# Differential attention: logits as float32 products over 64 rows instead of split products over 128

## The chip, the cores and the metric

The kernel runs on one core of a Trainium2 chip. The metric is the device time of one execution in microseconds (us); smaller is better. TensorE (PE) multiplies, VectorE (DVE) and ScalarE (ACT) work on tiles and empty PSUM, GpSimd (POOL) copies, and the queue of SyncE (SP) issues DMAs.

## The reference, cut to what matters

Two blocks run one after the other on x of 512 tokens by 1024 features, all in float32. The second block has two layers; its second layer is a differential attention with 8 heads of two sides each, a side having 64 features:

```python
q = q.reshape(B, S, B_HEADS, 2, HEAD_DIM_2) * (HEAD_DIM_2 ** -0.5)   # 8 heads, 2 sides, 64 features
k = k.reshape(B, S, B_HEADS, 2, HEAD_DIM_2)
v = v.reshape(B, S, B_HEADS, 2 * HEAD_DIM_2)
...
logits = jnp.einsum('bqhjd,bkhjd->bhjqk', q_blk, k).astype(jnp.float32) + bias[None]
p = jax.nn.softmax(logits, axis=-1)
a = p[:, :, 0] - lam_full * p[:, :, 1]
return jnp.einsum('bhqk,bkhe->bqhe', a.astype(v.dtype), v)
...
o = rms_norm(o, subln_g) * (1.0 - lambda_init)
```

For each head, side and tile of 128 queries the logits are a product of 128 by 512 over only 64 features.

## The kernel before

The stages follow one another: `mix`, `mlp1`, `A`, `mlpA`, `B`, `mlpB`. The change is in `B`, the function `layer_b`. Activations lie feature-major (128 features by 512 tokens in a tile). The precise products are made of fp32r pieces: `split` writes a value's fp32r copy (hi) and the rest (lo), and `mm3` adds hi*hi, hi*lo and lo*hi. The weights come as blocks in a fixed order (`_plan`, a class `Stream` with `take`); a block of 256 columns is loaded by the SP queue into `raw` (two buffers) and split by ACT (`hi`, L251) and DVE (`lo`, L252) into two pieces of 128 columns. `project` makes one tile of 128 columns by 512 tokens with 24 such products (`ps_pj`, three PSUM banks).

Everything else that PE writes in the layer (logits, transposes, attention output) takes its bank from one pool of five (`pwt`, tag `w`). Per head `hh` the steps are:

- `proj` (q, k, v; one block is two heads). DVE empties the bank with the norm's scale. A q tile is split (ACT L1338, DVE L1339) so that one half of the 128 rows holds a side's hi and the other half its lo. A k tile is split and copied so that both halves hold the side's hi (`KH`, ACT L1351 and POOL L1352) or its lo (`KL`, DVE L1353 and POOL L1354). v is turned token-major by PE (`ps_tm`).
- `soft`: for each of four query tiles and two sides, two products of 128 rows into one bank (`ps_lgb`: KH, then KL added). DVE adds the bias and takes the row's minimum while it empties the bank (L1378; q carries a minus sign), ACT takes the exponent with row sums (L1380), then reciprocal and scales (L1382, L1383), ACT scales side 1 (L1384) and DVE adds both sides (L1385). The bias tiles `bt` (448 KB each, three buffers) come by the SP queue (L1364).
- `pvb`: 16 transposes of the weights (`ps_aT`), copies by DVE and ACT, 16 products with v (`ps_ob`), squares on ACT (L1413), a reciprocal root of a dozen small DVE operations (L400 to L410) and a scaling by DVE (`ob`, L1417).
- `turn_out`: 4 transposes of `ob` (`ps_obT`), then a split by ACT (L279, `mh`) and DVE (L280, `ml`).

`B_STEPS` lists the steps in program order (q, k, v with the block number, s, p, t with the head). A scheduler turns it into one order per engine, fixed at build time: the earlier step goes first among those that it believes ready, so that projection products also stand between the pieces of other steps. On the chip each engine follows its order and waits on semaphores.

In layer `A` (`softmax_pair`, L1053) the logits are already float32 products over 64 rows, two heads in turn: per query tile 192, 256, 256 and 192 columns in the first three pairs of heads and 128 columns in the other five.

Of the kernel before, what the change touches and what calls it, by code (L numbers as in the profile page):

```python
# [16 lines left out]
P = 128  # L17
T = 512
# [9 lines left out]
A_STEPS = "q0 k0 s0 v0 t0 q1 p0 k1 s1 v1 t1 q2 p1 k2 s2 q3 t2 k3 s3 v2 t3 a0 p2 v3 p3".split()  # L28
B_STEPS = ("q0 k0 s0 v0 s1 p0 q1 t0 p1 k1 t1 s2 v1 s3 p2 q2 t2 p3 k2 t3 s4 v2 s5 p4 q3"
           " t4 p5 k3 t5 s6 s7 v3 p6 p7 t6 t7").split()  # L30
OH_B, OH_1, OH_2, OH_3 = 0, 1024, 1408, 1664
# [26 lines left out]
def _plan():  # L58
# [14 lines left out]
    for l, nm, steps in ((0, "a", A_STEPS), (1, "b", B_STEPS)):  # L73
        for t in steps:
            if t[0] in "qkv":
                out.append(_w_cols(nm + "_w_qkv_2", 0, {"q": 0, "k": 1024, "v": 2048}[t[0]] + int(t[1]) * 256))
        out += _w_out(nm + "_w_o_2", 0, 0, D)
        for half in range(2):
            out += [_w_cols("mlp_w_in_2", l, c) for c in range(half * 2048, (half + 1) * 2048, 256)]
            out += _w_out("mlp_w_out_2", l, half * 2048, (half + 1) * 2048)  # L80
# [89 lines left out]
def build(nc, tc, a, out, phases=("mix", "mlp1", "A", "mlpA", "B", "mlpB")):  # L170
# [814 lines left out]
    def rev(ap):  # L985

        return bass.AP(ap.tensor, ap.offset + P - 1, [list(ap.ap[0]), [P, 4], [-1, P]])
# [306 lines left out]
    def layer_b(st, biasd):  # L1294
# [24 lines left out]
        M_["evac"] = None  # L1319
        qs, ks, vs, at, ob = {}, {}, {}, {}, {}  # L1320

        def proj(i2, nm):
            wb = ws.take()
            for i in range(2):
                hh = 2 * i2 + i
                ps = project(wb[i:i + 1], x)  # L1330
                t = sp.tile([P, T], F32, tag="sq", name=nm)
                if nm == "q":
                    V.scalar_tensor_tensor(out=rev(t), in0=v4(ps), scalar=-0.125, in1=v4(st.rs), op0=ALU.mult,
                                           op1=ALU.mult)
                    qs[hh] = [gp.tile([P, T], F32R, tag="Q", name="Q", bufs=5) for _ in range(2)]
                    for j in range(2):
                        n, o = half[j], half[1 - j]
                        act(out=qs[hh][j][n, :], in_=t[n, :], func=AF.Copy)  # L1338
                        V.tensor_tensor(out=qs[hh][j][o, :], in0=t[n, :], in1=qs[hh][j][n, :].bitcast(F32),  # L1339
                                        op=ALU.subtract)  # L1340
                    continue
                V.tensor_tensor(out=t, in0=ps, in1=st.rs, op=ALU.mult)
                if nm == "v":
                    vs[hh] = gp.tile([P, T], F32, tag="vt", name="vt", bufs=4)
                    token_major(vs[hh], t)
                    continue
                kh = [gp.tile([P, T], F32R, tag=f"KH{j}", name="KH", bufs=2) for j in range(2)]
                kl = [(gp, sp)[j].tile([P, T], F32R, tag=("KL", "hold")[j], name="KL", bufs=2) for j in range(2)]
                for j in range(2):
                    n, o = half[j], half[1 - j]  # L1350
                    act(out=kh[j][n, :], in_=t[n, :], func=AF.Copy)  # L1351
                    G.tensor_copy(kh[j][o, :], t[n, :])  # L1352
                    V.tensor_tensor(out=kl[j][n, :], in0=t[n, :], in1=kh[j][n, :].bitcast(F32), op=ALU.subtract)  # L1353
                    G.tensor_copy(kl[j][o, :], kl[j][n, :].bitcast(F32))  # L1354
                ks[hh] = (kh, kl)

        half = (slice(0, 64), slice(64, P))

        def soft(hh):
            kh, kl = ks[hh]  # L1360
            bt = []
            for j in range(2):
                b = gp.tile([P, 896], F32, tag="bt", name="bt", bufs=3)
                nc.sync.dma_start(b, bass.AP(bv.tensor, bv.offset + (2 * hh + j) * OH_N + OH_B, [[1, P], [1, 896]]))  # L1364
                bt.append(b)
            mn = sp.tile([P, 2, 4], F32, tag="bmn", name="bmn")
            ss = sp.tile([P, 2, 4], F32, tag="bss", name="bss")
            rc = sp.tile([P, 2, 4], F32, tag="brc", name="brc")
            A = []
            for t in range(4):  # L1370
                Lt = []
                ts = slice(t * P, (t + 1) * P)
                for j in range(2):
                    ps = pwt("ps_lgb")
                    mm(ps, qs[hh][j][:, ts], kh[j], True, False)
                    mm(ps, qs[hh][j][:, ts], kl[j], False, True)
                    L = gp.tile([P, T], F32, tag=f"L{j}", name="Lb", bufs=8 if j == 0 else 2)
# [9 lines left out]
                A.append(Lt[0])  # L1387
            at[hh] = A

# [40 lines left out]

        for step in B_STEPS:
            nm, n = step[0], int(step[1])
            if nm in "qkv":
                proj(n, nm)
            elif nm == "s":
                soft(n)
            elif nm == "p":
                pvb(n)
            else:
                turn_out(n)  # L1440
# [177 lines left out]
```

## Time and profile before

| | us |
|---|---|
| time, median of 3 runs | 1919.89 |
| the runs | 1911.01 to 1925.99 |
| the profiled execution's own time | 1911.74 |
| its span, first to last instruction | 1910.0 |

The profile is of one execution. Busy times are sums over instructions; a PE record's end is modelled and reaches into the next one, so that the pace of PE is read from one start to the next. A float32 product shows as two records (two passes), an fp32r product and a transpose as one. The idle time of an engine stands in brackets with what ended it.

### The profile page before, as it was taken

To read this page: it belongs to the slowest core of one execution; us is meant where nothing else is said; L and a number is where in the kernel's file an instruction comes from. 1 tells how busy PE (TensorE), PEld (TensorE's weight loads), DVE (VectorE), ACT (ScalarE), POOL (GpSimd) and SP (SyncE) were. 2 spreads that over 40 slices of the span, in tenths; PEclk is the share of its full clock that TensorE was granted. 3 is DMA by queue.
4 is the path that set the end of the run, shared out by engine and by line. 5 is a ranking of instruction groups with operands and counts; after the bars stand their busy time and mean duration, and the time that the engine had idled before them with its cause. 6 is when DMAs were issued, how large, how long until landed. Compare 5 with 4: busy or idle time off the path is not lost.

```text
span 1910.0 us, 23525 instructions
## 1 busy us (share of the span) xinstructions
PE 1875.1 (98%) x9219; PEld 1541.2 (81%) x9219; DVE 1110.6 (58%) x2109; ACT 765.3 (40%) x1350; POOL 143.1 (7%) x136
## 2 busy tenths in 40 slices
PE   7999999999999999999999999999999999999997
PEld 5887878788888887787888888888888888888886
DVE  6795756666356666568543344457877754334433
ACT  5533334344234444354332134336656543213322
POOL 1232210011001103000000000001111000000000
PEclk9999999999999999999999999999999999999999
DMA  5231213222332234222332222343222222322221
GB/s 192 79 116 56 71 48 121 90 94 73 104 110 100 71 116 145 79 80 83 107 108 89 101 98 89 133 138 109 102 82 86 94 100 89 108 91 91 108 89 44
DMA packets 39646, 185.53 MB, mean 97 GB/s; under 512 B 9055, under 2 KB 10847, under 8 KB 22000
## 3 DMA queue, kind: packets, MB, share of 16 engines
q1 hardware_dynamic: 37552, 177.45, 26.6%
q0 software_dynamic: 1984, 6.59, 1.0%
q8 instruction: 72, 1.18, 0.2%
q14 instruction: 38, 0.31, 0.0%
HBM read 176.31 MB, written 7.71 MB: 96 GB/s over the span
## 4 chain that ended last, share of the span: by engine, by line
PE 55%; DVE 3%; ACT 1%; issue 1%; DVEq 0%; ACTq 0%
PE ps_pj L188 49%; PE ps_ob L188 1%; PE ps_lgb L188 1%; PE ps_po L188 1%; PE ps_aT L1396 1%; ACT junk L1413 0%; PE ps_lg L188 0%; DVE lo L252 0%; PE ps_bc L188 0%; DVE KL L1353 0%; DVE nb L408 0%; DVE nb L409 0%; PE ps_obT L1425 0%; PE ps_pT L1149 0%; PE ps_mean L188 0%
## 5 line engine op out<-in xcount | busy, mean ns | idle before, releaser
L188 PE MATMUL ps_pj<-xh,hi 128*128 128x512 f32 x1504 | 592.2, 394 | 11.9 <-ACT hi L251 11.0
L188 PE MATMUL ps_pj<-xl,hi 128*128 128x512 f32 x1504 | 590.9, 393 | 0.0
L188 PE MATMUL ps_pj<-xh,lo 128*128 128x512 f32 x1504 | 590.5, 393 | 0.0
L251 ACT ACTIVATE hi<-raw 128x1024 fp32r<-128x1024 f32 (+2 forms) x308 | 317.2, 1031 | 635.0 <-PE ps_pj L188 595.8
L252 DVE TENSOR_TENSOR lo<-raw,hi 128x1024 fp32r<-128x1024 f32 (+2 forms) x308 | 370.4, 1204 | 301.8 <-ACT hi L251 300.7
L188 PEld LDWEIGHTS ps_pj<-xh,hi 128*128 128x128 f32 x1504 | 283.1, 188 | 70.7 <-ACT hi L251 11.2
L188 PEld LDWEIGHTS ps_pj<-xh,lo 128*128 128x128 f32 x1504 | 283.1, 188 | 58.2 <-DVE lo L252 1.1
L188 PEld LDWEIGHTS ps_pj<-xl,hi 128*128 128x128 f32 x1504 | 283.2, 188 | 56.8 <-DVE xl L280 0.6
L188 PE MATMUL ps_pj<-ah,lo 128*128 128x512 f32 (+1 forms) x704 | 271.0, 385 | 0.0
L188 PE MATMUL ps_pj<-al,hi 128*128 128x512 f32 (+1 forms) x704 | 270.7, 385 | 0.2 <-DVE al L277 0.2
L188 PE MATMUL ps_pj<-ah,hi 128*128 128x512 f32 (+1 forms) x704 | 270.9, 385 | 0.0
L188 PEld LDWEIGHTS ps_pj<-al,hi 128*128 128x128 f32 x704 | 132.3, 188 | 26.8 <-DVE al L277 0.5
L188 PEld LDWEIGHTS ps_pj<-ah,hi 128*128 128x128 f32 x704 | 132.3, 188 | 26.5 <-ACT ah L276 0.4
L188 PEld LDWEIGHTS ps_pj<-ah,lo 128*128 128x128 f32 x704 | 132.3, 188 | 26.0
L469 DVE TENSOR_TENSOR ot<-ps_pj,r 128x512 f32<-128x512 f32 x31 | 21.5, 692 | 108.1 <-PE ps_pj L188 108.1
L188 PE MATMUL ps_pj<-mh,hi 128*128 128x512 f32 x192 | 74.8, 394 | 1.0 <-ACT mh L276 0.9
L276 ACT ACTIVATE ah<-ms 128x512 fp32r<-128x512 f32 x64 | 40.4, 632 | 87.4 <-DVE ms L974 86.0
L188 PE MATMUL ps_pj<-ml,hi 128*128 128x512 f32 x192 | 74.4, 392 | 0.6 <-DVE ml L277 0.6
L188 PE MATMUL ps_pj<-mh,lo 128*128 128x512 f32 x192 | 74.0, 390 | 0.0
L277 DVE TENSOR_TENSOR al<-ms,ah 128x512 fp32r<-128x512 f32 x64 | 44.3, 692 | 45.0 <-ACT ah L276 45.0
L947 DVE SCALAR_TENSOR_TENSOR my<-ms,cols,my 128x511 f32<-128x511 f32 (+1 forms) x88 | 65.6, 748 | 2.8 <-ACT my L945 1.3
L1380 ACT ACTIVATE Lb<-Lb,bmn 128x512 f32<-128x512 f32 x64 | 45.6, 713 | 13.9 <-DVE bmn L1378 11.6
(341 smaller groups left out, 1880.8 us busy)
## 6 DMA issues: line engine op xcount, KB each, us to landing
raw<-w_all SPq DMA_DIRECT2D x137, 1024.0 KB
bt<-biasd SPq DMA_DIRECT2D x16, 448.0 KB
raw<-w_all SPq DMA_DIRECT2D x8, 768.0 KB
raw<-w_all SPq DMA_DIRECT2D x8, 640.0 KB
hscr<-h POOLq DMA_DIRECT2D x16, 256.0 KB, 2.4
hold<-hscr SPq DMA_DIRECT2D x16, 256.0 KB
hs<-x_t SPq DMA_DIRECT2D x8, 256.0 KB
hold<-x_t SPq DMA_DIRECT2D x8, 256.0 KB
```

What stands on the lines that cost most here:

```text
L188: return nc.tensor.matmul(o, lhsT=l, rhs=r, start=start, stop=stop)
L251: act(out=hv, in_=iv, func=AF.Copy)
L252: i_lo = V.tensor_tensor(out=lv, in0=iv, in1=hv.bitcast(F32), op=ALU.subtract)
L276: act(out=dst_hi, in_=src, func=AF.Copy)
L277: V.tensor_tensor(out=dst_lo, in0=src, in1=dst_hi.bitcast(F32), op=ALU.subtract)
L469: V.tensor_tensor(out=t, in0=ps, in1=scale_row, op=ALU.mult)
L947: V.scalar_tensor_tensor(out=y[:, jj:], in0=s[:, :T - jj], scalar=col(base + m), in1=y[:, jj:], op0=ALU.mult, op1=ALU.add)
L1380: act(out=L, in_=L, func=AF.Exp, scale=-1.0, bias=mn[:, j, t:t + 1], accum_out=ss[:, j, t:t + 1])
L1396: nc.tensor.transpose(ps[:, t * P:(t + 1) * P], A[t][:, kt * P:(kt + 1) * P], ident)
```

## The change

`q` and `k` are no longer split. DVE writes them from PSUM straight into float32 tiles (`Q`, `K`, four buffers each), and each logit tile is one float32 product over the 64 rows of its side: side 0 lies on rows 0 to 63, side 1 on rows 64 to 127. The products of two query tiles form a group of four, the sides in turn, in a written order (`chain`), which stands behind the projection product issued last before it in program order (`in_order`; orders on PE, no semaphores). `soft` is cut in two (`s`: query tiles 0 and 1, `u`: 2 and 3), `proj` into its two tiles (`a`, `b`), and `B_STEPS` puts groups between them. The order of the weight blocks stays. ACT's and DVE's work on the logits is the same.

```diff
-B_STEPS = ("q0 k0 s0 v0 s1 p0 q1 t0 p1 k1 t1 s2 v1 s3 p2 q2 t2 p3 k2 t3 s4 v2 s5 p4 q3"
-           " t4 p5 k3 t5 s6 s7 v3 p6 p7 t6 t7").split()
+B_STEPS = ("q0a q0b k0a k0b s0 v0a u0 v0b s1 p0 q1a u1 q1b t0 p1 k1a k1b t1 s2 v1a u2 v1b s3 p2 q2a u3 q2b t2 p3"
+           " k2a k2b t3 s4 v2a u4 v2b s5 p4 q3a u5 q3b t4 p5 k3a s6 k3b t5 u6 v3a s7 v3b u7 p6 p7 t6 t7").split()
...
-        def proj(i2, nm):
-            wb = ws.take()
-            for i in range(2):
+        def proj(i2, nm, tile_):
+            if tile_ == "a":
+                wts[nm] = ws.take()
+            for i in ("ab".index(tile_),):
                 hh = 2 * i2 + i
-                ps = project(wb[i:i + 1], x)
-                t = sp.tile([P, T], F32, tag="sq", name=nm)
+                ps = project(wts[nm][i:i + 1], x)
                 if nm == "q":
-                    V.scalar_tensor_tensor(out=rev(t), in0=v4(ps), scalar=-0.125, in1=v4(st.rs), op0=ALU.mult,
+                    qs[hh] = gp.tile([P, T], F32, tag="Q", name="Q", bufs=4)
+                    V.scalar_tensor_tensor(out=rev(qs[hh]), in0=v4(ps), scalar=-0.125, in1=v4(st.rs), op0=ALU.mult,
                                            op1=ALU.mult)
-                    qs[hh] = [gp.tile([P, T], F32R, tag="Q", name="Q", bufs=5) for _ in range(2)]
-                    for j in range(2):
-                        n, o = half[j], half[1 - j]
-                        act(out=qs[hh][j][n, :], in_=t[n, :], func=AF.Copy)
-                        V.tensor_tensor(out=qs[hh][j][o, :], in0=t[n, :], in1=qs[hh][j][n, :].bitcast(F32),
-                                        op=ALU.subtract)
...
+                elif nm == "k":
+                    ks[hh] = gp.tile([P, T], F32, tag="K", name="K", bufs=4)
+                    V.tensor_tensor(out=ks[hh], in0=ps, in1=st.rs, op=ALU.mult)
...
-                    act(out=kh[j][n, :], in_=t[n, :], func=AF.Copy)
-                    G.tensor_copy(kh[j][o, :], t[n, :])
-                    V.tensor_tensor(out=kl[j][n, :], in0=t[n, :], in1=kh[j][n, :].bitcast(F32), op=ALU.subtract)
-                    G.tensor_copy(kl[j][o, :], kl[j][n, :].bitcast(F32))
...
+            for t in (2 * part, 2 * part + 1):
                 Lt = []
-                ts = slice(t * P, (t + 1) * P)
+                if t % 2 == 0:
+                    lg, seq = [], []
+                    for u in (t, t + 1):
+                        for j in range(2):
+                            lg.append(pwt("ps_lgb"))
+                            seq.append(mm(lg[-1], q[half[j], u * P:(u + 1) * P], k[half[j], :]))
+                    chain(seq)
+                    in_order(before, seq[0])
                 for j in range(2):
-                    ps = pwt("ps_lgb")
-                    mm(ps, qs[hh][j][:, ts], kh[j], True, False)
-                    mm(ps, qs[hh][j][:, ts], kl[j], False, True)
+                    ps = lg.pop(0)
```

`before` is PE's last projection product when `soft` is called. The two `bt` tiles of a head are requested in part 0 and used until the end of part 1.

## Rows read from the trace of the kernel before

**Rows 1.** The page, its part on busy time (us, share of the span, instructions) and the head of the chain that ended last.

```profile
PE 1875.1 (98%) x9219; PEld 1541.2 (81%) x9219; DVE 1110.6 (58%) x2109; ACT 765.3 (40%) x1350; POOL 143.1 (7%) x136
...
PE 55%; DVE 3%; ACT 1%; issue 1%; DVEq 0%; ACTq 0%
```

**Rows 2.** Stretches of layer B, each two heads long: length, then busy time of PE, its weight loads, DVE, ACT and POOL (instructions in brackets), granted clock, DMA share and GB/s.

```profile
1356.26:1411.17 54.91, 53.65 (x291) 44.76 (x290) 43.52 (x110) 35.21 (x78) 8.34 (x8) 1.00 0.27 92
1411.17:1466.07 54.90, 53.63 (x291) 44.76 (x290) 43.52 (x110) 35.20 (x78) 8.34 (x8) 1.00 0.27 92
```

**Rows 3.** The waits of PE from 1276 to 1507 us: who waited for whom, us in total, times, longest.

```profile
PE ps_obT L1425 <- DVE ob L1417: 3.1, 6, 0.7
PE ps_lgb L188 <- DVE ml L280: 0.6, 3, 0.2
```

**Rows 4.** PE in order of time, four places in layer B: start, us, what, idle time before it.

```profile
1337.43 0.39 PE L188 MATMUL ps_pj<-xh,lo 128*128 128x512 f32 x1
1338.19 0.66 PE L1425 MATMUL ps_obT<-ident,ob 128*128 128x128 f32 x4 [0.38 <-DVE ob L1417]
...
1354.84 0.39 PE L188 MATMUL ps_pj<-xh,lo 128*128 128x512 f32 x1
1355.88 0.63 PE L1425 MATMUL ps_obT<-ident,ob 128*128 128x128 f32 x4 [0.65 <-DVE ob L1417]
...
1414.71 0.39 PE L188 MATMUL ps_pj<-xl,hi 128*128 128x512 f32 x1
1415.31 0.50 PE L188 MATMUL ps_lgb<-KH,Q 128*128 128x512 f32 x1 [0.21 <-DVE ml L280]
...
1488.49 0.39 PE L188 MATMUL ps_pj<-mh,hi 128*128 128x512 f32 x1
1488.72 0.60 PE L436 MATMUL ps_tm<-ident,v 128*128 128x128 f32 x4
```

**Rows 5.** PE in order of time: the first of a run of 16 logit products and what follows the last of them, then a run of 26 records of float32 products over the whole array and what follows it.

```profile
1318.45 0.48 PE L188 MATMUL ps_lgb<-KH,Q 128*128 128x512 f32 x1
...
1322.23 0.38 PE L1396 MATMUL ps_aT<-ident,Lb 128*128 128x128 f32 x2
...
1327.45 3.06 PE L188 MATMUL ps_ob<-vt,aT 128*128 128x128 f32 x26
1330.27 0.47 PE L188 MATMUL ps_pj<-xl,hi 128*128 128x512 f32 x1
```

**Rows 6.** PE in order of time in layer A, around two groups of 64-row float32 logits (16 records, 8 products in a group).

```profile
728.78 0.39 PE L188 MATMUL ps_pj<-xh,lo 128*128 128x512 f32 x1
729.10 1.78 PE L188 MATMUL ps_lg<-k,q 64*128 64x192 f32 x16
730.81 0.50 PE L188 MATMUL ps_pj<-xh,hi 128*128 128x512 f32 x1
731.15 0.40 PE L188 MATMUL ps_pj<-xl,hi 128*128 128x512 f32 x1
...
819.30 0.39 PE L188 MATMUL ps_pj<-xh,lo 128*128 128x512 f32 x1
819.62 1.16 PE L188 MATMUL ps_lg<-k,q 64*128 64x128 f32 x16
...
821.05 0.39 PE L188 MATMUL ps_pj<-xl,hi 128*128 128x512 f32 x1
```

**Rows 7.** PE's instructions by line and shape, the logits of layer A: rows x columns of the stationary side, shape of the moving side, records, busy us, mean ns.

```profile
L188 PE MATMUL ps_lg<-k,q 64*128 64x128 f32 x80 | 5.8, 285 | 0.0
...
L188 PE MATMUL ps_lg<-k,q 64*128 64x192 f32 x24 | 3.3, 349 | 0.0
...
L188 PE MATMUL ps_lg<-k,q 64*128 64x256 f32 x24 | 3.1, 376 | 0.0
```

**Rows 8.** Instructions by line and shape from 1356.26 to 1411.17 us (two heads): busy us, mean ns, idle time before them.

```profile
L1353 DVE TENSOR_TENSOR KL<-k,KH 64x512 fp32r<-64x512 f32 x4 | 3.0, 760 | 0.5 <-ACT KH L1351 0.4
L1339 DVE TENSOR_TENSOR Q<-q,Q 64x512 fp32r<-64x512 f32 x4 | 2.7, 686 | 0.3 <-ACT Q L1338 0.2
...
L1352 POOL CAST KH<-k 64x512 fp32r<-64x512 f32 x4 | 5.0, 1253 | 46.3 <-DVE fc L410 45.4 <-DVE k L1342 0.8
```

**Rows 9.** All engines in order of time from 1410 us on: the first logit product of a head and what DVE did until it emptied the first bank.

```profile
1411.17 0.47 PE L188 MATMUL ps_lgb<-KH,Q 128*128 128x512 f32 x1
...
1412.76 1.71 DVE L1353 TENSOR_TENSOR KL<-k,KH 64x512 fp32r<-64x512 f32 x2 [0.39 <-ACT KH L1351]
...
1415.17 0.68 DVE L1378 CUSTOM_DVE_ANT_0 Lb<-ps_lgb,bt 128x512 f32<-128x512 f32 x1
```

**Rows 10.** DVE in order of time, two heads: the emptying of the first logit bank and the last operation of the head's second query tile.

```profile
1302.49 0.68 DVE L1378 CUSTOM_DVE_ANT_0 Lb<-ps_lgb,bt 128x512 f32<-128x512 f32 x1
...
1310.67 0.75 DVE L1385 SCALAR_TENSOR_TENSOR Lb<-Lb,brc 128x512 f32<-128x512 f32 x1 [0.20 <-ACT Lb L1384]
...
1319.24 0.69 DVE L1378 CUSTOM_DVE_ANT_0 Lb<-ps_lgb,bt 128x512 f32<-128x512 f32 x1
...
1326.05 0.75 DVE L1385 SCALAR_TENSOR_TENSOR Lb<-Lb,brc 128x512 f32<-128x512 f32 x1
```

**Rows 11.** The SP queue in order of time: a head's bias loads and the weight load behind them.

```profile
1364.16 4.25 SPq L1364 DMA_DIRECT2D bt<-biasd  x2
1374.26 0.33 SPq L243 DMA_DIRECT2D raw<-w_all  x1
```

More of the change, by code (lines that the diff above doesn't have):

```diff
@@ L74, in _plan @@
         for t in steps:
-            if t[0] in "qkv":
+            if t[0] in "qkv" and t[2:] != "b":
                 out.append(_w_cols(nm + "_w_qkv_2", 0, {"q": 0, "k": 1024, "v": 2048}[t[0]] + int(t[1]) * 256))
@@ L1319, in layer_b @@
         M_["evac"] = None
-        qs, ks, vs, at, ob = {}, {}, {}, {}, {}
-        def proj(i2, nm):
-            wb = ws.take()
-            for i in range(2):
+        qs, ks, vs, at, ob, wts, bts, sts = ({} for _ in range(8))
+        def proj(i2, nm, tile_):
+            if tile_ == "a":
+                wts[nm] = ws.take()
+            for i in ("ab".index(tile_),):
                 hh = 2 * i2 + i
-                ps = project(wb[i:i + 1], x)
-                t = sp.tile([P, T], F32, tag="sq", name=nm)
+                ps = project(wts[nm][i:i + 1], x)
@@ L1341, in proj @@
-                    continue
-                V.tensor_tensor(out=t, in0=ps, in1=st.rs, op=ALU.mult)
-                if nm == "v":
+                elif nm == "k":
+                    ks[hh] = gp.tile([P, T], F32, tag="K", name="K", bufs=4)
+                    V.tensor_tensor(out=ks[hh], in0=ps, in1=st.rs, op=ALU.mult)
+                else:
+                    t = sp.tile([P, T], F32, tag="sq", name=nm)
+                    V.tensor_tensor(out=t, in0=ps, in1=st.rs, op=ALU.mult)
                     vs[hh] = gp.tile([P, T], F32, tag="vt", name="vt", bufs=4)
@@ L1345, in proj @@
                     token_major(vs[hh], t)
-                    continue
-                kh = [gp.tile([P, T], F32R, tag=f"KH{j}", name="KH", bufs=2) for j in range(2)]
-                kl = [(gp, sp)[j].tile([P, T], F32R, tag=("KL", "hold")[j], name="KL", bufs=2) for j in range(2)]
-                for j in range(2):
-                    n, o = half[j], half[1 - j]
-                    act(out=kh[j][n, :], in_=t[n, :], func=AF.Copy)
-                    G.tensor_copy(kh[j][o, :], t[n, :])
-                    V.tensor_tensor(out=kl[j][n, :], in0=t[n, :], in1=kh[j][n, :].bitcast(F32), op=ALU.subtract)
-                    G.tensor_copy(kl[j][o, :], kl[j][n, :].bitcast(F32))
@@ L1355, in proj @@
[L1355 to L1370, printed above, removed]
-                Lt = []
-                ts = slice(t * P, (t + 1) * P)
+        half = (slice(0, 64), slice(64, P))
@@ new lines, in soft @@
+        def soft(hh, part):
+            q, k = qs[hh], ks[hh]
+            before = M_["pe"]
+            if part == 0:
+                bt = bts[hh] = []
+                for j in range(2):
+                    b = gp.tile([P, 896], F32, tag="bt", name="bt", bufs=3)
+                    nc.sync.dma_start(b, bass.AP(bv.tensor, bv.offset + (2 * hh + j) * OH_N + OH_B, [[1, P], [1, 896]]))
+                    bt.append(b)
+                sts[hh] = [sp.tile([P, 2, 4], F32, tag=t, name=t) for t in ("bmn", "bss", "brc")]
+                at[hh] = []
+            bt, A = bts[hh], at[hh]
+            mn, ss, rc = sts[hh]
+            for t in (2 * part, 2 * part + 1):
+                Lt = []
+                if t % 2 == 0:
[6 more added lines that the diff above has]
+                    in_order(before, seq[0])
@@ L1387, in soft @@
                 A.append(Lt[0])
-            at[hh] = A
         def pvb(hh):
@@ L1433, in layer_b @@
             if nm in "qkv":
-                proj(n, nm)
-            elif nm == "s":
-                soft(n)
+                proj(n, nm, step[2])
+            elif nm in "su":
+                soft(n, "su".index(nm))
             elif nm == "p":
```

## The prediction

> **What bounds the kernel now.** I read the page first, then a stretch of two heads, then PE's waits there, then PE in order of time around each wait. PE is busy for 98% of the span and the chain that ended last runs mostly over PE [rows 1]. As a record's end is modelled, the other half of the argument is the pace: projection products start 0.227 us apart wherever nothing disturbs them. Layer B repeats every two heads: 54.9 us, with PE at full clock, DVE busy for 43.5 and ACT for 35.2 of it [rows 2]. So neither is the bound, but DVE with 79% is close enough to be late at single places. Such places are nearly all that PE loses: it waits six times for `ob` before the transposes of an output and three times for `ml` before logits [rows 3].
>
> What a wait costs is read from start to start, against the 0.23 us from a projection product to a transpose that does not wait (1488.49 to 1488.72) [rows 4]. The first kind takes 0.76, so it loses 0.53; the second 1.04, so 0.81; the wait for `ml` 0.60, so 0.37 [rows 4]. Together 1.71 us, three times over (the counts 6 and 3 of rows 3 are two and one in each of three repetitions): 5.1 us. That is the most that work off PE can give back. Everything else must come from PE's own work.
>
> **Term 1: the logits on PE.** Before, a head needs 16 fp32r products of 512 columns, four for each query tile. A run of 16 takes 3.78 us (1318.45 to 1322.23), 0.236 each; free of neighbours it would be the 0.227 of the projections [rows 4, 5]. The layer has 128 of them: 29.1 to 30.2 us.
>
> After, there are 16 groups of four float32 products, two pairs of sides. Layer A has the same form with other column counts, so its two kinds of group give a straight line. From the projection product before a group to the second one after it pass 2.37 us with 896 columns on each side (192, 256, 256 and 192) and 1.75 us with 512 (four times 128) [rows 6, 7]. Less two projection products (0.454) the group costs 1.92 and 1.30 us: 1.615 ns for each column of a side, and 0.47 us fixed. The fixed part is seen at the edges: 0.32 instead of 0.227 on the way in (728.78 to 729.10), 0.34 for the first projection product afterwards (730.81 to 731.15), the rest between the last record and the first [rows 6]. The new group has 1024 columns on each side (two query tiles of 512), so 1.65 + 0.47 = 2.12 us. No row has 512 columns at once; the line is drawn past its last point.
>
> 16 x 2.12 = 33.9 us against 29.1 to 30.2: +3.7 to +4.8. The change thus saves PE nothing: two sides at a quarter of the pace beside each other are worth four products at full pace, and the fixed part comes on top. Lower end: eight groups stand beside transposes, which are float32 too, and may share part of the way in and out. I allow 0.2 us for each (the two edges above, 0.09 and 0.11), so +2.1. I take +4.3, the middle without sharing.
>
> **Term 2: work taken off DVE, ACT and POOL.** For two heads DVE loses 4 subtractions for k (3.0 us) and 4 for q (2.7), and POOL its casts [rows 8]. None of it is on PE's path except through the waits above, so its worth is bounded by 5.1 us. Each wait has a reason that the change touches. In front of `ml`, DVE does two KL subtractions that take 1.71 us with the wait for ACT before them; they go, and 1.71 is more than the 0.37 [rows 4, 9]. The 0.81 kind (head 1 after k's tiles) has KL work between the small operations of the reciprocal root; two subtractions at 0.76 us are more than the wait too [rows 8]. The 0.53 kind has two q subtractions in it (2 x 0.69 us), but the new group `u` puts four bank emptyings of 0.68 us near the same place [rows 8, 9]. I count the first two fully (3 x 1.18 = 3.5) and half of the third (0.8): -4.3. The ends are -5.1 and 0.
>
> **Term 3: a new wait.** Before, the second half of head 1 is computed a whole block of q (48 products) ahead of its transposes; now `u1` has only `q1b` and `t0` behind it before `p1`. The same holds for `u3` and `u5`. Cover on PE: 2.12 for the group, 24 x 0.227 = 5.45 for the tile, some 0.45 for four transposes: 8.0 us. Need: two query tiles of softmax. In one head it took 7.6 us from the first bank to the end of the second tile (1319.24 to 1326.80), in another 8.9 (1302.49 to 1311.42), each starting 0.8 us after the first product [rows 5, 10]. That is 8.4 to 9.7 us, 0.4 to 1.7 too late, but both stretches hold banks of the other two tiles, which a half head does not have. Three places: 0 to +5.1; I take +0.4 in all. Behind the waiting transposes everything on PE stands still.
>
> **At nothing.** The emptying of q and k costs DVE the same as before, now straight into the tile, and the logits follow at least a projection tile (5.45 us) later. A group's order needs no semaphore. The bias loads of a head are held through its second part, so the second load of heads 1, 3, 5 and 7 can be issued only when the even head's `u` has freed a buffer: about 0.8 + 3 x 0.68 us after it starts, while its first use is at 2.12 + 5.45 + 0.8 + 0.7 = 9.1. This leaves some 6 us. Before, such a pair took 4.25 us to go out, the second one too waiting for its buffer [rows 11], and none of PE's waits hangs on it [rows 3]. Behind it in SP's queue is a weight load (1374.26), whose split comes a block later. If that cover is gone, DVE is late at the same places as in rival B. ACT and POOL lose only work.
>
> **Sum.** 4.3 - 4.3 + 0.4 = +0.4 us on the profiled execution's 1911.7: 1912.1. The profile was of a quick execution; the median of the runs is 8.2 us above it. On the scale of the medians: 1919.9 + 0.4, rounded to 1920.
>
> **Rivals.**
> A, better: the groups share their switches (+2.1), all waits go (-5.1) and none is new: -3.0, 1909 by the profile, 1917 on the medians' scale. For it speaks that DVE loses 5.7 of 43.5 us in a stretch.
>
> B, slower: the banks. A group takes four of the pool's five banks at once; the next user at `s1`, `s3`, `s5` and `u7` is `pvb`, whose first transposes take the fifth. Its second set, at about 2.5 us (the group plus four transposes of 0.11), needs a bank that DVE has emptied, and nothing passes a waiting transpose on PE. It decides when DVE begins: the first bank is free 0.68 us after that, so up to 1.8 us after the first product costs nothing. In the trace it began after 0.8 us once (1318.45 to 1319.24) and after 4.0 us another time (1411.17 to 1415.17) [rows 5, 9, 10]. At 4.0 the wait is 2.2 us and each later set follows at DVE's pace, some 1 us more: 4 x 3.2 = +13, so 1925, or 1933. Against it: the 4.0 were mostly KL work, which goes, and the old run of 16 products took eight banks in 3.8 us without a stop [rows 5].
>
> C, slower by more than 1%: the sides do not run beside each other at 512 columns. Each group takes 1.65 us longer, 16 x 1.65 = +26.5: 1939, or 1947. Against it: 16 records of 224 columns on average take 1.71 us in layer A (729.10 to 730.81), while one after the other, at the 0.84 ns a column of a product over the whole array (2.82 us for 26 records of 128 columns), they would take 3.0 [rows 5, 6]. For it: no row with a full bank for each side.
>
> D, between: the sides hinder each other in part, say a quarter of the pace is lost at 512 columns. 1.65 / 0.75 is 0.55 more per group, +8.8: 1921, or 1929. The rows give no sign of it up to 256 columns, where a column's pass costs 0.81 ns against 0.84 over the whole array [rows 5, 6]. The Trainium skill (TensorE: Matmul & The Clock Gate, Measured speedup) reports 3.07 times, not 4, for four row tiles at 512 columns, which speaks against this change; by that rule a group would take 0.50 us longer and the sum would be some 8 us more. No run here has shown that count of columns.
>
> E, it does not do what it says: the scheduler parts the groups, as it parted the old logits into pairs, and each half pays the fixed part: 16 x 0.47 = +7.5, so 1920, or 1928.
>
> **How the numbers follow.** The forecast has 0.62, A 0.14, B 0.11, D 0.06, C 0.04, E 0.03. The bounds of the terms give 2.1 - 5.1 + 0 = -3.0 and 4.8 + 0 + 5.1 = +9.9. With the scatter of the runs about their median (-8.9, +6.1) that is 1908 to 1936, which takes in A, B, D and E and leaves out C. About 1% (19.2 us) is what a measurement of this kernel can tell from no change. Faster than that would need more than twice the waits that exist: 0.02, for scatter. Slower than that is C, and B together with D: 0.07. The rest is 0.91.
>
> **What would show it.** The logits appear as 128 records of 64 rows by 512 columns, in 16 groups of 8, each group 2.1 us from the projection product before it to the second one after it, less two. A pair's pass should take near 0.415 us from start to start; 0.83 is C, 0.55 is D. PE's waits for `ob` should fall from 3.1 us to under 1 and those for `ml` vanish. New waits of PE for `Lb` at `p1`, `p3` and `p5` are term 3; waits of transposes for banks that L1378 empties are B. DVE should lose 5.7 us in a stretch of two heads, which should still be 54 to 56 us long. The prediction is wrong if that stretch moves by more than 3 us, or if time moves outside layer B.

## The result and the profile after

The changed kernel takes 1926.82 us (median of 20 runs, 1918.69 to 1934.7), the kernel before 1912.1 in the runs beside it (20 runs, 1910.39 to 1925.99): a ratio of 1.0059, with a 95% interval of 1.0042 to 1.0075. It is slower by about 0.6%, where +0.4 us was forecast. The time lies in the range, and the change within 1%; the size is wrong, and the next sections find out which term. One execution of the kernel before took 3818.45 us, in the runs beside e1 to e4 below; it is left out of every ratio and median here.

The profiled execution took 1927.0 us with a span of 1925.2, so 15.2 us longer than the span of 1910.0 before. Of the page, first, the line of busy times that answers to [rows 1]:

```profile
PE 1887.5 (98%) x9219; PEld 1533.8 (80%) x9219; DVE 1086.1 (56%) x2077; ACT 747.4 (39%) x1318; POOL 111.1 (6%) x104
```

DVE, ACT and POOL have lost work, as the change says (24.5, 17.9 and 32.0 us). PE's busy time has grown by 12.4, and that is two things of different kinds. The first lies far ahead of the change, in `mix`, and shows in the windows of one stretch: first of the kernel before, then of the changed one (length, busy time of PE, weight loads, DVE, ACT, POOL, granted clock, DMA share, GB/s).

```profile
252.00:270.00 18.00, 17.80 (x166) 13.27 (x164) 8.58 (x22) 7.39 (x19) 0.00 (x0) 1.00 0.17 60
```

```profile
252.00:270.00 18.00, 18.00 (x126) 13.16 (x127) 5.43 (x15) 3.72 (x12) 0.00 (x0) 0.53 0.17 60
```

PE was granted 0.53 of its clock where it had 1.00: the lower level, 1.2 GHz, for nearly the whole stretch. It gets through 126 instructions in the time of 166. Up to the start of layer B this costs 6.7 us, in code that the change does not touch; the instruction orders of DVE and ACT up to layer B are the same in both traces. The second thing is layer B itself. It is measured from the products of its first mean. Two ends are used: the first product after the last transposes of an output, which the expectations below go by, and the first product of the next mean, behind the output projection. First the kernel before, then the changed one:

```profile
1281.71 1.02 PE L188 MATMUL ps_mean<-inv_d,acc 128*128 128x1 f32 x8
...
1507.10 0.48 PE L188 MATMUL ps_pj<-mh,hi 128*128 128x512 f32 x1
...
1546.42 1.02 PE L188 MATMUL ps_mean<-inv_d,acc 128*128 128x1 f32 x8
```

```profile
1288.40 1.02 PE L189 MATMUL ps_mean<-inv_d,acc 128*128 128x1 f32 x8
...
1521.04 0.48 PE L189 MATMUL ps_pj<-mh,hi 128*128 128x512 f32 x1
...
1561.74 1.02 PE L189 MATMUL ps_mean<-inv_d,acc 128*128 128x1 f32 x8
```

To the first end that is 225.39 us before and 232.64 after, +7.25. But this end does not stand at the same place in the work: of the 192 products of the output projection 36 lie ahead of it before and 30 after, and the six that are left over cost 6 x 0.227 = 1.4 us behind it. The second end has all 192 ahead of it in every kernel: 264.71 us before and 273.34 after, +8.63. With the 6.7 that makes up the 15.2 to 0.1 us; nothing is lost behind layer B. So two questions are open: is the clock in `mix` the change's doing, and where do the 8.6 us come from?

The clock first. The runs of either kernel fall into three groups by the mean clock that each run lists, near 0.998, 0.993 and 0.988, and the medians of neighbouring groups lie about 7 us apart, as the 6.7 us above suggest. The traces agree: the changed kernel's first profile, at 0.993, has one stretch of 17 us at the lower clock in `mix`, its second one (e7, at 0.987) has two, and that of the kernel before, at 0.998, has none. By the clocks that the runs list, both kernels have all three groups. In the run of the unchanged and the changed kernel side by side described below (e7), the groups compare as follows, in us:

| mean clock | before | after | difference |
|---|---|---|---|
| about 0.998 | 1911.4 (17 runs) | 1919.5 (6 runs) | +8.1 |
| about 0.993 | 1918.2 (9 runs) | 1925.9 (4 runs) | +7.8 |
| about 0.988 | 1925.0 (9 runs) | 1934.2 (2 runs) | +9.1 |

At equal clock the change costs 8 to 9 us, which is what layer B alone shows in the trace. In the first comparison 7 of 20 runs of the changed kernel had the highest clock and 13 of 20 of the kernel before, and 8 against 1 the lowest, the groups of the kernel before being told there by the times alone; in e7 the shares come closer (6 of 12 against 17 of 35 at the highest, 2 against 9 at the lowest). So the part of the median's 14.7 us above the 8 to 9 is a difference in how often the lower clock came. Whether the change makes it come more often is not settled by this many runs. From here on the time of layer B and the medians at the highest clock are compared.

Now layer B. The repeated stretch of two heads, in the form of [rows 2]:

```profile
1364.93:1421.53 56.60, 54.96 (x289) 41.60 (x288) 37.07 (x101) 30.76 (x71) 0.00 (x0) 1.00 0.27 89
```

56.60 us instead of 54.90, at full clock, with less work on every engine but PE: DVE 37.1 instead of 43.5, ACT 30.8 instead of 35.2. PE's waits through the layer, in the form of [rows 3]:

```profile
PE ps_ob L189 <- DVE aT L1394: 4.4, 4, 1.1
PE ps_tm L437 <- DVE v L1340: 1.7, 5, 0.3
PE ps_obT L1418 <- DVE ob L1410: 0.5, 1, 0.5
PE ps_lgb L189 <- DVE K L1337: 0.3, 1, 0.3
PE ps_aT L1389 <- DVE Lb L1379: 0.2, 1, 0.2
```

The old waits for `ob` (3.1 us, six times, at `t0` to `t5`) are gone, and so are those for `ml`; the one for `ob` that is left stands at `t6`, where the kernel before had none. In their place stand two that no row of before showed: PE's first product with v waits for the first copy of the turned weights (`aT`), and v's transposes wait for v. One place in the stretch shows both. PE in order of time:

```profile
1381.49 0.39 PE L189 MATMUL ps_pj<-xh,hi 128*128 128x512 f32 x1
1382.21 0.63 PE L437 MATMUL ps_tm<-ident,v 128*128 128x128 f32 x4 [0.33 <-DVE v L1340]
1382.77 1.99 PE L189 MATMUL ps_lgb<-K,Q 64*128 64x512 f32 x8
1384.69 1.96 PE L1389 MATMUL ps_aT<-ident,Lb 128*128 128x128 f32 x16
1387.77 0.49 PE L189 MATMUL ps_ob<-vt,aT 128*128 128x128 f32 x2 [1.11 <-DVE aT L1394]
1388.01 0.48 PE L189 MATMUL ps_pj<-xl,hi 128*128 128x512 f32 x1
```

And DVE over the same microseconds:

```profile
1380.05 1.41 DVE L1379 SCALAR_TENSOR_TENSOR Lb<-Lb,brc 128x512 f32<-128x512 f32 x2 [0.25 <-ACT Lb L1378]
1381.39 0.68 DVE L1340 TENSOR_TENSOR v<-ps_pj,rs 128x512 f32<-128x512 f32 x1
...
1383.93 0.69 DVE L1372 CUSTOM_DVE_ANT_0 Lb<-ps_lgb,bt 128x512 f32<-128x512 f32 x1 [0.73 <-PE ps_lgb L189]
...
1386.22 0.17 DVE L1376 RECIPROCAL brc<-bss 128x2 f32<-128x2 f32 x1 [0.36 <-ACT Lb L1374]
1386.34 0.69 DVE L1372 CUSTOM_DVE_ANT_0 Lb<-ps_lgb,bt 128x512 f32<-128x512 f32 x1
...
1387.03 0.68 DVE L1394 COPY aT<-ps_aT 128x512 f32<-128x512 f32 x1
```

The second wait is read like this. PE does the group of `s3`, then turns the weights of head 2 for `p2` from 1384.69 on (the first repetition has the same with `s1` and `p0`). DVE has the four emptyings of that group (from 1383.93 to 1387.03; two are shown) ahead of the copy of the turned weights, because `s3` is the earlier step; between the third and the fourth it also stands 0.36 us for ACT, since a small operation of the softmax is ahead in its order. It begins the copy at 1387.03, 2.3 us after the first of the 16 transposes and well after the four that the copy needs, and PE, which has finished all sixteen by 1386.5, stands until 1387.77. From start to start the first product comes 1.27 us later than 16 transposes at 0.11 us would let it; in four places that is 5.1 us. The first wait is the same thing earlier: v's emptying at 1381.39 stands behind two additions of the half head `u2`, whose group came a projection tile earlier, and the transposes start 0.72 us after the projection product ahead of them instead of 0.23 [rows 4]. It costs 0.49 here and 0.30 at the other v of the stretch; over the layer's eight v tiles (0.15 to 0.50 each) it comes to 3.2 us. Together 8.3 us that the sum did not have.

The groups themselves came out as the rows of layer A said. PE around one that stands between projection products:

```profile
1339.57 0.39 PE L189 MATMUL ps_pj<-xh,lo 128*128 128x512 f32 x1
1339.89 1.99 PE L189 MATMUL ps_lgb<-K,Q 64*128 64x512 f32 x8
1341.80 0.50 PE L189 MATMUL ps_pj<-xh,hi 128*128 128x512 f32 x1
1342.14 0.40 PE L189 MATMUL ps_pj<-xl,hi 128*128 128x512 f32 x1
```

From 1339.57 to 1342.14 are 2.57 us, less two projection products (0.454): 2.12 us. Inside, by the starts of the single records, the two sides' passes start 7 ns apart, and the next two 0.43 us later.

### The profile page after: what moved, and what is told of

Same layout as the page of the kernel before. It is cut to its first block, busy times and chain, and to the rows that moved or that the text cites. A ratio compares the mean times of both kernels' runs of the same rounds, so it can differ in the third digit from the quotient of the medians.

```text
span 1925.2 us, 23372 instructions
## 1 busy us (share of the span) xinstructions
PE 1887.5 (98%) x9219; PEld 1533.8 (80%) x9219; DVE 1086.1 (56%) x2077; ACT 747.4 (39%) x1318; POOL 111.1 (6%) x104
## 4 chain that ended last, share of the span: by engine, by line
PE 54%; DVE 3%; ACT 2%; issue 1%; DVEq 0%; ACTq 0%
PE ps_pj L189 49%; PE ps_ob L189 1%; ACT Lb L1374 1%; PE ps_lgb L189 1%; PE ps_po L189 1%; DVE Lb L1379 1%; ACT Lb L1378 0%; DVE Lb L1372 0%; PE ps_lg L189 0%; PE ps_aT L1389 0%; PE ps_bc L189 0%; PE ps_tm L437 0%; DVE v L1340 0%; PE ps_pT L1150 0%; PE ps_mean L189 0%
```

## The experiments

The theory tested (theory 1) is that the order of steps costs, through the two new waits, and that the product costs what term 1 says and no more. Against it stand two others: that the products of 64 rows hinder each other or their neighbours, and that DVE is late wherever the emptyings of a group come, whatever the order. Besides each kernel's ratio with its interval, layer B's time in the profile is given, to the first of the two ends above (before 225.39, after 232.64), as the expectations use it, and the median at the highest mean clock (before 1911.4 beside e1 to e7, 1910.6 beside e8 and e9). As that end stands at different places in the work (25 to 39 of the 192 products ahead of it), kernels are compared by the second one, the next mean:

| kernel | layer B, first end | to the next mean | against the kernel before |
|---|---|---|---|
| before | 225.39 | 264.71 | |
| changed (e7) | 232.64 (232.69) | 273.34 (273.37) | +8.6 (+8.7) |
| e1 | 230.55 | 269.17 | +4.5 |
| e2 | 246.28 | 288.07 | +23.4 |
| e3 | 229.62 | 270.74 | +6.0 |
| e4 | 228.98 | 269.65 | +4.9 |
| e6a | 223.67 | 264.80 | +0.1 |
| e6b | 223.93 | 264.15 | -0.6 |
| e5 | 228.71 | 270.52 | +5.8 |
| e8 | 252.30 | 290.95 | +26.2 |
| e9 | 220.94 | 261.78 | -2.9 |

In e1 and e2 PE ran at the lower clock in part of the layer, as told there; in the others the layer had 1.00 throughout.

**The new steps with the old product (e1).** The steps, the halves and the tile-by-tile projections of the changed kernel, but q and k are split as before and each logit tile is two fp32r products:

```diff
-                    qs[hh] = gp.tile([P, T], F32, tag="Q", name="Q", bufs=4)
...
+                    qs[hh] = [gp.tile([P, T], F32R, tag="Q", name="Q", bufs=5) for _ in range(2)]
...
-                            seq.append(mm(lg[-1], q[half[j], u * P:(u + 1) * P], k[half[j], :]))
+                            ts = slice(u * P, (u + 1) * P)
+                            seq.append(mm(lg[-1], qs[hh][j][:, ts], kh[j], True, False))
+                            seq.append(mm(lg[-1], qs[hh][j][:, ts], kl[j], False, True))
```

> The new step order, cut tiles and half softmaxes, but q and k split as before and four fp32r products of 128 rows for each query tile; nothing is left out. Measured on layer B alone: from the norm's mean products in front of it to the end of its last output transposes, 225.4 us in the kernel before and 232.6 in the changed one. Theory 1 (the order costs it: v's transposes in front of the groups, and DVE emptying four banks in front of the copies for p0, p2, p4, p6): the new waits of PE are there with the old products too, about +8, and the old waits go only in part since DVE keeps its splitting: 228 to 232 us. Theory 2 (the float32 products cost it): 225 to 226 us.

Layer B 230.55 us, ratio 1.002 (0.9991 to 1.005), 1914.4 at the highest clock, +3.0 over the kernel before. The layer's time is inside what theory 1 gave, but through another wait than it named. PE's waits in layer B:

```profile
PE ps_obT L1433 <- DVE ob L1425: 4.2, 5, 2.0
PE ps_lgb L189 <- POOL KH L1352: 0.8, 1, 0.8
...
```

With the splits back on DVE it is `ob` that comes late again, once by 2.0 us, and behind that one PE ran at the lower clock for some 3.4 us. The wait for `aT` that theory 1 named is not there at all. So the order by itself is not free, but which wait it brings depends on the work left on DVE.

**The new product in the old order (e2).** The change's product and its halves, but both halves of a head stand together where the head's logits stood before:

```diff
-B_STEPS = ("q0a q0b k0a k0b s0 v0a u0 v0b s1 p0 q1a u1 q1b t0 p1 k1a k1b t1 s2 v1a u2 v1b s3 p2 q2a u3 q2b t2 p3"
+B_STEPS = ("q0a q0b k0a k0b s0 u0 v0a v0b s1 u1 p0 q1a q1b t0 p1 k1a k1b t1 s2 u2 v1a v1b s3 u3 p2 q2a q2b t2 p3 ...
```

> The float32 products and unsplit q and k, but in the old step order: both halves of a head's softmax one behind the other, then whole blocks. Theory 1 (the order costs it): the products cost some 3 us more than the old ones, the old waits (5.1 us) go with the splitting, and the second group of each head waits a little for banks: layer B takes 223 to 227 us. Theory 2 (the products cost it): 231 to 233 us.

Layer B 246.28 us, ratio 1.0109 (1.0065 to 1.0154), 1934.5 to 1942: the expectation was far off. PE's waits:

```profile
PE ps_aT L1388 <- DVE bmn L1371: 6.7, 3, 2.2
PE ps_tm L436 <- DVE v L1339: 3.7, 3, 1.3
...
```

The first line is rival B's wait, from twice its burst: eight logit tiles in a row out of a pool of five banks, and the transposes of the head before wait for a bank that DVE has not emptied. PE in order of time there, and the window around it:

```profile
1388.30 4.26 PE L188 MATMUL ps_lgb<-K,Q 64*128 64x512 f32 x16
1392.62 1.34 PE L1388 MATMUL ps_aT<-ident,Lb 128*128 128x128 f32 x8
1396.19 0.66 PE L1388 MATMUL ps_aT<-ident,Lb 128*128 128x128 f32 x4 [2.24 <-DVE bmn L1371]
...
1390.00:1400.00 10.00, 7.67 (x35) 5.21 (x33) 8.40 (x29) 8.74 (x21) 0.00 (x0) 0.88 0.50 169
```

Behind two of the three waits of 2.24 us (those that ended at 1334.90 and 1396.19) PE worked at the lower clock for 3.41 us; behind the third, which ended at 1457.46, the granted clock stayed at 1.00. A third such stretch began at 1500.0, behind waits of 0.34 and 0.81. So parting a head into halves with a projection tile between them is what makes these groups bearable: to the next mean the new order saves 14.7 us against the old one with the same products, of which some 5 are the lower clock (an estimate: half the pace for three times 3.41 us). If DVE's emptyings cost the same in whatever order, this kernel and the changed one would agree.

**v's transposes moved behind the next group (e3).** A new step `m` turns v after the next half head's group, so that nothing on PE waits for v's emptying:

```diff
-... s0 v0a u0 v0b s1 p0 ...
+... s0 v0a u0 m0 v0b s1 m1 p0 ...
-                    token_major(vs[hh], t)
+                    vraw[hh] = t
...
+            elif nm == "m":
+                token_major(vs[n], vraw[n])
```

> The changed kernel with v's transposes one step later, behind the group of logits that follows the v tile. Theory 1: PE's waits for DVE's v tile (0.30 and 0.49 us beyond an undisturbed step, in each of four repetitions) go, since the group of 1.9 us stands in between: layer B 232.6 - 3.1 = 229.5 us. If these waits only move to the next thing PE needs from DVE: 232 to 233 us.

Layer B 229.62 us (229.5 expected), ratio 1.0035 (1.0006 to 1.0064), 1917.1 at the highest clock. To the next mean this kernel is 2.6 us quicker than the changed one, by the first end 3.0. The wait for v is gone; the one for `aT` has turned into two smaller ones further up, the first of them for a bank, as in rival B:

```profile
PE ps_aT L1388 <- DVE bmn L1371: 1.1, 4, 0.3
PE ps_aT L1388 <- DVE Lb L1378: 1.0, 3, 0.3
```

**The heads' outputs one tile later (e4).** `p0`, `p2` and `p4` behind the next projection tile, so that DVE has done the four emptyings when PE turns the weights:

```diff
-... v0b s1 p0 q1a u1 q1b ...
+... v0b s1 q1a p0 u1 q1b ...
```

> The changed kernel with p0, p2 and p4 one projection tile later, so that DVE has emptied the four banks of s1, s3, s5 when the transposes of p come. Theory 1: the wait of PE's first output product for DVE's copy (1.27 us beyond an undisturbed step) goes at three of its four places: 232.6 - 3.8 = 228.8 us for layer B. Rival: p then stands close before u and t, and the wait comes back at the output transposes, 232 us or more.

Layer B 228.98 us (228.8 expected), ratio 1.0032 (1.0002 to 1.0062), 1916.5. The waits left are v's, and one for `aT` at the end of the layer, where no tile is left to put between:

```profile
PE ps_tm L436 <- DVE v L1339: 2.0, 7, 0.4
PE ps_ob L188 <- DVE aT L1393: 1.1, 1, 1.1
```

**Both (e6a), and the last head's too (e6b).** e6a is e3 and e4 together; in e6b `p6` also stands ahead of `u7`:

```diff
-... k3a s6 k3b t5 u6 v3a s7 v3b u7 p6 p7 t6 t7
+... k3a s6 k3b t5 u6 v3a s7 m6 v3b p6 u7 m7 p7 t6 t7
```

> The changed kernel with v's transposes behind the next group and p0, p2, p4 one projection tile later: both edits of the two experiments before. They took 3.0 and 3.7 us off layer B. Theory 1 (each wait is its own): 232.6 - 6.7 = 226 us for layer B, within 1 us of the kernel before, ratio 0.999 to 1.003. Rival (the waits are one backlog of DVE and show up elsewhere): 228 to 230 us, ratio 1.002 to 1.004.

> As the one before, and at the layer's end p6 stands in front of u7. If the copy wait at p6 (1.3 us in the changed kernel) goes and output projection products cover the softmax of u7: layer B 224 to 225.5 us. If p7 then waits for u7's softmax (8 us behind its start, with little but the output projection to fill): 226 to 230 us.

e6a: layer B 223.67 us, less than the 226 expected; ratio 0.9988 (0.9962 to 1.0015), 1912.0 at the highest clock. To the next mean each edit alone gave 2.6 and 3.7 us; together they take 8.5 off the changed kernel, near the 8.3 that the two waits were read to cost. Alone, each left the other wait standing or brought new ones. e6b: 223.93 us, 0.9983 (0.9956 to 1.0009), 1910.3, no clear step beyond e6a. The largest of PE's waits in e6b, which are 1.2 us in all:

```profile
PE ps_lgb L188 <- DVE K L1336: 0.4, 1, 0.4
PE ps_aT L1388 <- DVE bmn L1371: 0.3, 1, 0.3
...
```

That is theory 1: with v's transposes and three heads' outputs moved in the order of steps, the same float32 products give a kernel level with the one before. The orders were changed in two ways at once, so DVE's order at other places moved as well, and 8.5 is not to be split to a tenth.

**The changed kernel once more (e7)**, as the comparison for these.

> The changed kernel itself, unaltered, in the same rounds. It tells how its executions stand to those of the kernel before when both are sorted by the mean granted clock. Layer B: 232.6 us. If the change is responsible only for layer B, executions at the highest clock lie 7 to 9 us above those of the kernel before at theirs, and the lower clocks (half speed in an unchanged stage) come in both kernels, as often in one as in the other. If the change brings the lower clocks about: they come more often here.

Layer B 232.69 us, ratio 1.0024 (0.9997 to 1.0051); the table above is from this set. The layer's time repeats to 0.05 us; by the groups of clock above, the ratio differs from the first one through how often each clock came.

**Side 0 twice, then side 1 twice (e5).** Only the order inside a group:

```diff
-                            seq.append(mm(lg[-1], q[half[j], u * P:(u + 1) * P], k[half[j], :]))
+                    for j in range(2):
+                        for u in (t, t + 1):
+                            seq.append(mm(lg[2 * (u - t) + j], q[half[j], u * P:(u + 1) * P], k[half[j], :]))
```

> The changed kernel with a group's four products in another order: both query tiles of side 0, then both of side 1. If the sides overlap only where they stand in turn, the second product must wait for the first (same rows), the third runs beside the second, and the fourth waits again: three product times of 0.83 us in place of two, so a group costs some 2.95 us in place of 2.12 and layer B 232.6 + 16 x 0.83 = 246 us. If the order of issue does not matter: 232 to 233 us. If the sides did not overlap in the changed kernel either: 232 to 233 us too, but then a pair's pass would show twice the 0.43 us from start to start.

```profile
1388.43 0.39 PE L189 MATMUL ps_pj<-xh,lo 128*128 128x512 f32 x1
1388.75 1.99 PE L189 MATMUL ps_lgb<-K,Q 64*128 64x512 f32 x8
...
1391.01 0.40 PE L189 MATMUL ps_pj<-xl,hi 128*128 128x512 f32 x1
```

The group takes 2.13 us as before (2.58 less 0.454), not the 2.95 expected: this was meant to take the overlap away and did not. The records start in pairs 13 ns apart instead of 7. So it says nothing on what the overlap is worth. It shows that the two halves of the rows ran beside each other though the products of one half stood first in PE's order: the order is the kernel's, as a record does not tell its half, but products of one half alone never start in pairs (e8, next). Layer B is 228.71 us all the same (1.0015, 0.9986 to 1.0045; 1917.6), because DVE's order came out otherwise: the copy of the turned weights stands ahead of some emptyings, and PE's waits for it are smaller:

```profile
PE ps_ob L189 <- DVE aT L1396: 2.2, 4, 0.6
PE ps_ob L189 <- ACT aT L1394: 0.9, 4, 0.3
```

Why an order inside the group moved DVE's copy was not pursued.

**One side in a group (e8).** A half head is now the four query tiles of one side instead of two tiles of both, so that no product has the other half of the rows beside it. Nothing is left out:

```diff
-            for t in (2 * part, 2 * part + 1):
...
+            j = part
+            lg, seq = [], []
+            for t in range(4):
+                lg.append(pwt("ps_lgb"))
+                seq.append(mm(lg[-1], q[half[j], t * P:(t + 1) * P], k[half[j], :]))
```

> The changed kernel with groups of one side: part s makes the four query tiles of side 0, part u those of side 1; the same 64 products of 64 rows, but none of the other side near it. The experiment with the sides apart within a group left the group's time as it was (2.12 us), which two readings allow. Reading 1 (the two halves of the rows work beside each other whatever the order within a group): here nothing can overlap, a group takes 2048 x 1.615 ns + 0.47 = 3.8 us, layer B 232.6 + 16 x 1.65 = 259 us less some waits that the longer groups hide, 252 to 260; a product's pass starts 0.43 us after the one before, alone. Reading 2 (a 64-row product is as quick by itself, and the sides in turn give nothing): a group stays at 2.1 us and layer B at 230 to 236 us.

```profile
1395.84 0.39 PE L189 MATMUL ps_pj<-xh,lo 128*128 128x512 f32 x1
1396.16 3.70 PE L189 MATMUL ps_lgb<-K,Q 64*128 64x512 f32 x8
...
1400.13 0.40 PE L189 MATMUL ps_pj<-xl,hi 128*128 128x512 f32 x1
```

3.84 us for the same group of eight records (4.29 less 0.454) against 2.12, with 0.43 us for each pass in either. Layer B 252.3 us (252 to 260 expected), ratio 1.0142 (1.0116 to 1.0167). This is rival C made to happen: 16 x 1.71 = 27 us of overlap, all of which the changed kernel has. So the sides do not hinder each other. To the next mean the layer rose by 17.6 us over the changed kernel and not by 27, since behind a group of 3.8 us the waits for `aT` and v are gone; only waits of 0.3 for K and 0.2 for `ob` are left.

**The old product, in a better order (e9).** If the gain of term 2 was the removal of old waits, then they may go by order alone. The kernel before, with only `t0` to `t5` one step later:

```diff
-B_STEPS = ("q0 k0 s0 v0 s1 p0 q1 t0 p1 k1 t1 s2 v1 s3 p2 q2 t2 p3 k2 t3 s4 v2 s5 p4 q3"
-           " t4 p5 k3 t5 s6 s7 v3 p6 p7 t6 t7").split()
+B_STEPS = ("q0 k0 s0 v0 s1 p0 q1 p1 t0 k1 s2 t1 v1 s3 p2 q2 p3 t2 k2 s4 t3 v2 s5 p4 q3"
+           " p5 t4 k3 s6 t5 s7 v3 p6 p7 t6 t7").split()
```

> The kernel before, with its split products, and only its step list changed: the output transposes t0 to t5 one step later (behind the next p or s). Its nine waits of PE in layer B (5.1 us beyond undisturbed steps) stand before the output transposes and, through their bank, before logits. If they are a matter of order alone: layer B 225.4 - 5 = 220 to 221.5 us, ratio 0.997 to 0.998, below every kernel with float32 logits. If they come from DVE's splitting work, which stays: 224 to 226 us.

Layer B 220.94 us (220 to 221.5 expected). PE's waits there:

```profile
PE ps_ob L188 <- ACT aT L1399: 1.4, 3, 0.5
PE ps_obT L1425 <- DVE ob L1417: 0.3, 1, 0.3
```

The ratio is 0.9987 (0.997 to 1.0004), and at equal clock 1908.7 against 1910.6 and 1914.9 against 1917.3. It has the shortest layer B of all kernels here, but to the next mean it gains 2.9 us on the kernel before and not the 4.5 that the first end shows: the old waits went, and the smaller ones above came. A gain of some 2 us in the whole time is likely but not proven, as the interval takes in 1.

## Why the prediction was right in its range and wrong in its sum

**The range held in part by luck.** The median after, 1926.82, lies in 1908 to 1936. The upper bound of +9.9 had room for the +8.63 only because it held 5.1 us for term 3, a wait that did not come; two waits that no term named took that room. The 1920 also stands on a median of three runs, 1919.9, where twenty runs beside the changed kernel gave 1912.1; on that base the same sum would have read 1912.5.

**Term 1, the logits on PE: right.** The group was put at 2.12 us by a line drawn past its last point, and measures 2.12; beside transposes it is read at 2.1 to 2.2, so the shared switch is not seen. A pair's pass takes 0.429 us where 0.415 stood. From start to start, waits left out, all 16 groups with their edges take 34.3 us and the 128 old products 31.0, where 29.1 to 30.2 was taken: +3.3. Between two kernels in which hardly any wait is left, e6b with float32 products (264.15 to the next mean) and e9 with the split ones (261.78), it is +2.4, or +2.9 when the waits on record are taken off each (1.2 and 1.7). Forecast was +4.3 with bounds of 2.1 and 4.8. On this kernel the change makes PE's own work longer.

**Term 2, the old waits: right.** -4.3 was forecast. The waits for `ml` went as said, and all six for `ob` went too, 5.1 us in all; the one for `ob` on record afterwards stands at `t6`, at the layer's end, where the kernel before had none. But e9 shows that these waits did not need the change: with `t0` to `t5` one step later nearly all of them went, the splits in place.

**Term 3, the wait for u's softmax: nothing** at `p1`, `p3` and `p5`, where 0.4 was taken of 0 to 5.1. The one wait for `Lb`, 0.2 us, stands at the layer's end, and the kernel before has one of 0.2 there too.

**What failed: the sum lacked two waits, 8.3 us.** 3.3 - 5.1 + 8.3 is 6.5, and to the next mean the layer shows 8.63. Another 1.7 is read, from start to start, at smaller waits that are new as well: ACT's copy of the turned weights (three times 0.2), `ob` at `t6` (0.7) and K (0.4). About 0.4 us stays unassigned. The first and larger of the two, 5.1 us, is a cousin of rival B. The prediction saw that four emptyings stand ahead of the transposes of `pvb` and asked only when a bank comes free; it gave that 0.11. It put the price on the wrong user. The fifth bank and DVE's start after about 1.2 us were enough for the transposes, which never waited for a bank in the changed kernel. But the next step of the same chain, the copy of the turned weights, is itself DVE work and queued behind the same four emptyings. At this place a wait for a bank would have ended with the first emptying, 0.69 us after 1383.93; the wait for DVE's copy ended behind all four, at 1387.03 and the copy's 0.68 us. The second, 3.2 us, was in no term: v's transposes are not named in the prediction at all, though `u` was put into the middle of block v, where it sets softmax work ahead of v's emptying. "The emptying of q and k costs DVE the same as before" was counted at nothing and was nearly so (0.3 us, once); v's was the one that mattered, because its user on PE follows at once and those of q and k follow a tile later.

The bound that the prediction named for the stretch, 3 us, was too wide to catch this: the stretch moved by 1.7, since its new waits (1.27 and 0.79, together 2.1 us) are largely set off there by the old ones that went (1.7); but the new ones come with each of the four pairs of heads, the old ones with three. DVE lost 6.4 us in the stretch, more than the 5.7 named, and still came late: its load was never the point, only what stands ahead of what.

**The rivals.** C is refuted by e8, D by the pass of 0.429 us and the group of 2.12. The Trainium skill (TensorE: Matmul & The Clock Gate, Measured speedup) has 3.07 times instead of 4 for four row tiles. With two row halves this case shows 3.84 us one side at a time against 2.12 in turn, and less the 0.47 us of fixed part that is 3.37 against 1.65, 2.04 times of 2. So that rule's loss does not appear here. E is absent from the changed kernel. In e6b the scheduler did part the groups of `u`, but between products that are float32 too, and no fixed part was paid twice. PE in e6b around such a group:

```profile
1341.64 1.13 PE L188 MATMUL ps_lgb<-K,Q 64*128 64x512 f32 x4
1342.70 3.39 PE L188 MATMUL ps_ob<-vt,aT 128*128 128x128 f32 x28
1346.02 1.13 PE L188 MATMUL ps_lgb<-K,Q 64*128 64x512 f32 x4
1347.08 0.50 PE L188 MATMUL ps_pj<-xh,hi 128*128 128x512 f32 x1
```

1.06 us for each half from start to start, 2.12 for both. A did not come, since new waits took the place of the old ones.

**Time outside layer B.** The prediction called itself wrong if time moved there, and 6.7 of the profile's 15.2 us did, all of it ahead of the layer. At equal clock the whole program differs by 7.8 to 9.1 us, layer B's 8.6 and little else, so the 6.7 belong to the clock that these executions were granted. That the change has no part in it was not shown.

## What to carry to other kernels

When a burst of work is moved between two steps, follow its emptyings in the queue of the engine that does them, up to the next instruction that the bound engine needs from that engine; the time when a buffer comes free is only the first of the dates to be compared. Where waits of the bound engine stand for a few microseconds in a stretch that repeats, try an order of steps first: here a few moved steps took away what the rewritten arithmetic had been credited with. An engine with a third of its time idle can be late at every single place that counts.

## What the runs showed of the hardware

Products on different halves of the rows ran beside each other at full pace at 512 columns of float32, 2.12 us against 3.84 for the same number on one half (e8), and they did so also when two products of one half were issued ahead of the two of the other (e5: 2.13 us, pairs 13 ns apart).

A short wait can cost more than its length, but need not: behind two of three waits of 2.24 us on PE (e2), and at the end of one of 1.99 us (e1), the granted clock fell from 2.4 to 1.2 GHz for about 3.4 us; behind the third wait of 2.24 us it stayed at 2.4 GHz. In `mix` it fell to the lower level and stayed there for some 17 us without a gap of more than 0.2 us on PE in the nine us before it, in a stretch of products of 32 rows by 32 columns; the kernel before did the same products ahead of it with the same gap and kept 1.00. What decided between the two executions is open.
